# Feature-major products of a decoder layer as three 256-column matmuls a weight tile

## The chip, the cores and the metric

The kernel runs on one core of one Trainium2 chip. The metric is the device time of one execution in microseconds (us); the median of several runs is given. A profile is one further execution, with every engine's instructions recorded. TensorE is shown there as PE (matmuls) and PEld (weight loads), VectorE as DVE, ScalarE as ACT, GpSimd as POOL, SyncE as SP.

## The reference

One decoder layer on 256 tokens of width 2048, all in float32: a half-step SwiGLU feed-forward network (FFN) with layer norm, a token mixer, and a second such FFN.

```python
def swiglu(h, w_in, w_out):
    a, b = jnp.split(h @ w_in, 2, axis=-1)
    return (jax.nn.silu(a) * b) @ w_out

h = layer_norm(DN_ALPHA * h + 0.5 * swiglu(h, ffn1_w_in, ffn1_w_out), ln1_g, ln1_b)
q, k, v, qi, ki, wi, rx, rg, gates = split_cols(h @ w_in)
...                                              # rotary positions
y_attn = dsa_attention(q, k, v, qi, ki, wi)      # 16 heads, 64 keys chosen for each query
y_rnn = rglru_branch(rx, rg, conv_w, conv_b, wa, ba, wx, bx, lam)
g_attn, g_rnn = jnp.split(jax.nn.sigmoid(gates), 2, axis=-1)
merged = g_attn * (y_attn @ w_attn_branch) + g_rnn * (y_rnn @ w_rnn_branch)
h = layer_norm(DN_ALPHA * h + merged @ w_out, ln2_g, ln2_b)
h = layer_norm(DN_ALPHA * h + 0.5 * swiglu(h, ffn2_w_in, ffn2_w_out), ln3_g, ln3_b)
```

The FFN is 5632 wide, the recurrent branch 2560.

## The kernel before

Every weight is read once from HBM, in 1 MB chunks, and passes through TensorE once. For accuracy each float32 operand is kept as two float32r parts, high and low (`split`, and L108/L109 in `Weights.split_to` for the weights: ACT writes the high part `wh`, DVE the low part `wl`, 1024 columns at a time). A product is the sum of three partial products: high by high, high by low, low by high.

`Weights.unit` hands out the weight tiles in the order in which TensorE takes them. When a piece of 1024 columns (eight tiles of 128) is used up, it has the piece that is three further on split (`AHEAD` = 3, four buffers each for `wh` and `wl`), and lets one stage of the background work (`Background.step`: attention heads, rotary, indexer, recurrence) be emitted. The order of PE, SP and POOL is that of the program (`manual_schedule`); the order on ACT and DVE is planned by the framework from its own costs.

There are two kinds of product. Token-major ones (`blockA`; the output products and the q, k, v, qi projections) have the tokens as stationary operand and stream 512 weight columns: three matmuls of 512 columns (L446 to L448) for each of the two token halves. Feature-major ones have the 128x128 weight tile as stationary operand and stream the 256 tokens; their result is the next operand without a transpose. An activation tile `x` is 128 x 2 x 256: high part, then low part.

For the feature-major ones the kernel has two forms. `mmB` (L417, L418) streams high and low tokens together as 512 columns by the high weights, so that the two partial products lie side by side in a PSUM bank, and then the 256 high tokens by the low weights onto the first half. `sumB` then copies the second half to SBUF on ACT (L469) and adds the first half to it on DVE (L471). `mm3` (L831 to L833) has three matmuls of 256 columns that all accumulate in the first half of a bank; nothing is left to add.

Which product has which form: `mmB` with `pairB`, two banks at a time, in both FFNs' first products (1408 weight tiles each; the two sums go through Silu and a product, L600, L601, and a split, L475, L476); `mmB` with `blockB` in the ki projection (16 tiles), the two gates (256 tiles each: `ga` with Tanh at L797, `gr` at L883), the attention branch (256, on `ya`, L802) and the recurrent branch (320, on `yr`, L890, L891). `mm3` with `block3` in the recurrent inputs rx and rg (640 tiles on `hs`) and with `xc` in the two recurrent gates (104 tiles). The operands are `xs` in FFN 1 and `hs` behind a layer norm in the mixer and in FFN 2. PSUM has four banks for the products (`MM`) and four for the background work (`BP`).

Of the kernel before, what the change touches and what calls it, by code (L numbers as in the profile page):

```python
# [11 lines left out]
AF = mybir.ActivationFunctionType  # L12
OP = mybir.AluOpType
AX = mybir.AxisListType.X

P = 128
# [44 lines left out]


class Weights:
    """The weight stream: DMA of whole chunks, exact split of each piece into two float32r
    parts, and the units of the products in the order in which TensorE takes them."""

    def __init__(self, nc, pool, chunks, on_piece):
        self.nc, self.pool, self.chunks, self.on_piece = nc, pool, chunks, on_piece
# [58 lines left out]


class Background:
    """Work that is emitted a stage at a time between the pieces of the weight stream."""  # L130

    def __init__(self):
        self.lanes = {}
# [21 lines left out]


class Lazy:
    """The K tiles of an operand, emitted group by group, `ahead` groups before their use."""

    def __init__(self, n, per, make, ahead=1):  # L160
        self.n, self.per, self.make, self.ahead = n, per, make, ahead
# [14 lines left out]
def tile_layer(ctx, tc, x_fm, x_tm, pos, f1a, f1o, wA, wki, wB, lru, wab, wrb, wo, f2a, f2o,  # L176
# [66 lines left out]

    W = Weights(nc, pool, chunks, bg.step)

    # ---- start: x, constants
    xraw = [U("x") for _ in range(NK // 2)]

    def load_x_fm(k2):
# [128 lines left out]

    bg.add("main", later(consts(), W.last.ins))

    # ---- residual stream, token-major: Y[t][nb]
    Y = [[None] * 4 for _ in range(2)]

    def load_x():
# [27 lines left out]
                V.scalar_tensor_tensor(y, br, ALPHA, y, op0=OP.mult, op1=OP.add)  # L412
                yield

    # ---- products
    def mmB(ps, x, w, first, last):
        T.matmul(ps, w[0], x.rearrange("p a t -> p (a t)"), start=first, stop=False)  # L417
        T.matmul(ps[:, :S], w[1], x[:, 0], start=False, stop=last)  # L418

    def blockB(x):  # L420
        ps = MM()
        for k in range(len(x)):
            mmB(ps, x[k], W.unit(P), k == 0, k == len(x) - 1)
        return ps

    def pairB(x):
        pa, pb = MM(), MM()
        n = len(x)
        for h in range(2):
            for ps in (pa, pb):  # L430
                for k in range(h * n // 2, (h + 1) * n // 2):
                    mmB(ps, x[k], W.unit(P), k == 0, k == n - 1)
        return pa, pb

    def blockA(x, finish=None, lag=0, hold=False):
        """`finish`: the first half of the tokens runs ahead over the last pieces, and its sums
        are handed to it before the second half takes them. `hold`: the weights of the next
        product wait until the end of this one is on its way."""
        ps = [MM(), MM()]
        n = len(x)  # L440

        def half(t, k, w):
            wh, wl = w
            xh = x[k][:, 0, t * P:(t + 1) * P]
            xl = x[k][:, 1, t * P:(t + 1) * P]
            T.matmul(ps[t], xh, wh, start=k == 0, stop=False)  # L446
            T.matmul(ps[t], xh, wl, start=False, stop=False)  # L447
            T.matmul(ps[t], xl, wh, start=False, stop=k == n - 1)  # L448

        lead = 2 * lag  # L450
        ranges = [(k, k + 2) for k in range(0, n, 2)]
        if finish:
            ranges = ranges[:-lag] + [(n - lead, n)]
        for k0, k1 in ranges:
            ws = []
            for k in range(k0, k1):
                if hold and k == n - 2 * AHEAD:
                    W.spare = AHEAD
                ws.append(W.unit(512))
                half(0, k, ws[-1])  # L460
            if finish and k1 == n:
                finish(ps)
            for k in range(k0, k1):
                half(1, k, ws[k - k0])
        return ps

    def sumB(ps):
        t = T1()
        A.activation(t, ps[:, S:], AF.Copy)  # L469
        s = T1()  # L470
        V.tensor_tensor(s, ps[:, :S], t, op=OP.add)  # L471
        return s

    def split(dst, f):
        A.activation(dst[:, 0], f, AF.Copy)  # L475
# [31 lines left out]
            self.chained(t)  # L507

    class InnerNorm(Norm):
        """Layer norm whose result is the next operand, split and feature-major."""  # L510

        def __init__(self, gk, bk, g, b):
            self.gk, self.bk, self.g, self.b = gk, bk, g, b
# [28 lines left out]
            return hs  # L542

    class OuterNorm(Norm):
        """The last layer norm: its result leaves token-major."""

        last = True

# [23 lines left out]
                    nc.sync.dma_start(out[t * P:(t + 1) * P, nb * 512:(nb + 1) * 512], Y[t][nb])  # L572

    def out_product(x, ln):
        """Y += 0.5 x W; with `ln`, on to the statistics of the layer norm that follows."""

        def done(nb, ps, t):
            y_add(ps, nb, ln, t)
            if ln and nb == 3:
                ln.chain(t)  # L580

        for nb in range(4):
            if ln and nb == 3:
                ps = blockA(x, lambda ps: done(3, ps, 0), LAG_LAST if ln.last else LAG_LN, not ln.last)
                done(3, ps, 1)
            else:
                ps = blockA(x)
                for t in range(2):
                    done(nb, ps, t)
        if ln and ln.last:  # L590
            ln.finish()

    def ffn(x, ln):
        for s in range(SEG):
            g = []
            for j in range(NKS):
                pa, pb = pairB(x)
                sa = sumB(pa)
                sb = sumB(pb)
                A.activation(sa, sa, AF.Silu)  # L600
                V.tensor_tensor(sb, sa, sb, op=OP.mult)  # L601
                hl = UHL("g")
                split(hl, sb)
                g.append(hl)
            if s == SEG - 1:
                new_stats()
                ln.prepare()
            out_product(g, s == SEG - 1 and ln)

    # ==== FFN 1  # L610
    ln = InnerNorm("ln1_g", "ln1_b", ln1_g, ln1_b)
    ffn(xs, ln)
    hs = ln.hs

    # ==== mixer: token-major part of the input projection
    qT, kT, v, qiT = [None] * 8, [None] * 2, [None] * 2, [None] * 4
    kiT = C([P, S], "kiT")
    wi = C([P, 2, NIH], "wi")
# [154 lines left out]
        bg.add("head", head(h), 3)  # L773
    for b in a_order:
        if b is None:
            bg.add("rope", ki_task(sumB(blockB(hs))))
            for t in range(2):
                bg.add("rope", indexer(t))
            continue
        ps = blockA(hs)  # L780
        stg = stage(ps)
        if b >= 6:
            bg.add("rope", heads_T(stg, qiT, (b - 6) * 2, 8))
        elif b == 5:
            v[0], v[1] = stg
        elif b == 4:
            bg.add("qk", heads_T(stg, kT, 0, 16))
        else:
            bg.add("qk", heads_T(stg, qT, 2 * b, 16))
    # ==== attention gate, attention branch  # L790
    ga = []
    for j in range(NK):
        s = sumB(blockB(hs))
        if j % 2 == 0:
            u = U("ga")
        d = u[:, (j % 2) * S:(j % 2 + 1) * S]
        A.activation(d, s, AF.Tanh, scale=0.5)  # L797
        ga.append(d)
    bg.drain("rope", "qk", "head")
    for j in range(NK):  # L800
        s = sumB(blockB(ya))
        V.scalar_tensor_tensor(ga[j], ga[j], 1.0, s, op0=OP.add, op1=OP.mult)  # L802
    ya = None

    # ==== recurrent branch
    yr = [None] * NR

    def recur(g, tiles):
# [18 lines left out]
            yr[g * TPG + c] = hl  # L827
            yield

    def mm3(ps, x, w, first, last):  # L830
        T.matmul(ps[:, :S], w[0], x[:, 0], start=first, stop=False)  # L831
        T.matmul(ps[:, :S], w[0], x[:, 1], start=False, stop=False)  # L832
        T.matmul(ps[:, :S], w[1], x[:, 0], start=False, stop=last)  # L833

    def block3(x):
        ps = MM()
        for k in range(len(x)):
            mm3(ps, x[k], W.unit(P), k == 0, k == len(x) - 1)
        return ps[:, :S]

    xgs, xcs, tiles = {}, {}, []
    for j in range(NR + LAG):
        if j < NR:
# [13 lines left out]
        if j >= LAG:  # L857
            i = j - LAG
            g, c = divmod(i, TPG)
            pr, pi = MM(), MM()  # L860
            for ps in (pr, pi):
                ks = LRU_K[c]
                for n, k in enumerate(ks):
                    mm3(ps, xcs[g * TPG + k], W.unit(P), n == 0, n == len(ks) - 1)
            vw = U("vw")
            r, t = T1(), T1()
            A.activation(r, pr[:, :S], AF.Tanh, scale=0.5, bias=hba[:, i:i + 1])
            A.activation(t, pi[:, :S], AF.Tanh, scale=0.5, bias=hbx[:, i:i + 1])
            A.activation(vw[:, :S], r, AF.Tanh, scale=sp2[:, i:i + 1], bias=sp2[:, i:i + 1])
            V.scalar_tensor_tensor(xgs[i][:, :S], t, 1.0, xgs[i][:, :S], op0=OP.add, op1=OP.mult)  # L870
            tiles.append((xgs[i], vw))
            if c == TPG - 1:
                bg.add("rec", recur(g, tiles))
                tiles = []

    # ==== recurrent gate, recurrent branch, merge
    gr = []
    for j in range(NK):
        s = sumB(blockB(hs))
        if j % 2 == 0:  # L880
            u = U("gr")
        d = u[:, (j % 2) * S:(j % 2 + 1) * S]
        A.activation(d, s, AF.Tanh, scale=0.5)  # L883
        gr.append(d)
# [1 line left out]
    bg.drain("rec")  # L886
    mg = []
    for j in range(NK):
        s = sumB(blockB(yr))
        V.scalar_tensor_tensor(s, gr[j], 1.0, s, op0=OP.add, op1=OP.mult)  # L890
        V.tensor_tensor(s, s, ga[j], op=OP.add)  # L891
        hl = UHL("mg")
        split(hl, s)
        mg.append(hl)
    yr = None

    # ==== output projection
    new_stats()
    ln = InnerNorm("ln2_g", "ln2_b", ln2_g, ln2_b)
    out_product(mg, ln)  # L900
    mg = None

    # ==== FFN 2
    ffn(ln.hs, OuterNorm(ln3_g, ln3_b))


# [72 lines left out]
```

## Time and profile before

| | |
|---|---|
| median of 3 runs | 2487.92 us (2487.12 to 2487.92) |
| span of the profiled execution | 2489.5 us (first to last instruction; no other time of it is recorded) |
| mean granted TensorE clock | 0.996 |
| PE busy | 2458.6 us (99%), 13700 matmuls |
| PEld busy | 2122.5 us (85%), 13700 weight loads |
| DVE busy | 1502.6 us (60%) |
| ACT busy | 1267.8 us (51%) |
| read from HBM | 458.87 MB, 185 GB/s over the span |

In the profile's rows an instruction is shown with its line in the kernel, its engine, its operation, what it writes and reads (`mm<-hs,wh`: PSUM tile mm from hs and wh), and its shape; `x1936` is how many there are. A row of a group then has the busy time in us and the mean of one in ns, and behind the next bar the idle time of the engine just before these instructions with what ended it. A row of one line's instructions has the shortest, median and longest duration in ns and then the first and last start in us. A row of the waits has who waited for whom, then the total in us, the number and the longest. A row of the timeline has start and duration in us. Matmuls overlap, so a matmul's duration is longer than the distance between the starts of two.

### The profile page before, as it was taken

To read this page: it belongs to the slowest core of one execution; us is meant where nothing else is said; L and a number is where in the kernel's file an instruction comes from. 1 tells how busy PE (TensorE), PEld (TensorE's weight loads), DVE (VectorE), ACT (ScalarE), POOL (GpSimd) and SP (SyncE) were. 2 spreads that over 40 slices of the span, in tenths; PEclk is the share of its full clock that TensorE was granted. 3 is DMA by queue.
4 is the path that set the end of the run, shared out by engine and by line. 5 is a ranking of instruction groups with operands and counts; after the bars stand their busy time and mean duration, and the time that the engine had idled before them with its cause. 6 is when DMAs were issued, how large, how long until landed. Compare 5 with 4: busy or idle time off the path is not lost.

```text
span 2489.5 us, 33942 instructions
## 1 busy us (share of the span) xinstructions
PE 2458.6 (99%) x13700; PEld 2122.5 (85%) x13700; DVE 1502.6 (60%) x2106; ACT 1267.8 (51%) x1821; POOL 44.2 (2%) x74
## 2 busy tenths in 40 slices
PE   8999999999999999999999999999999999999997
PEld 7888888888887778888999988887888888888886
DVE  7555445555556676655788875655755544555555
ACT  5544434444335455544688874444554533544432
POOL 0000000000002000000000000002000000000001
PEclk9999999999999999999999999999999999999999
DMA  7655555555555444455555555555555556555553
GB/s 270 222 185 187 172 190 196 186 186 186 181 191 192 171 162 152 151 180 182 176 183 191 179 209 186 186 186 191 181 187 193 187 186 228 186 190 191 186 186 110
DMA packets 70557, 463.16 MB, mean 186 GB/s; under 512 B 8032, under 2 KB 8032, under 8 KB 17792
## 3 DMA queue, kind: packets, MB, share of 16 engines
q1 hardware_dynamic: 68400, 454.59, 52.2%
q0 software_dynamic: 2000, 6.41, 0.9%
q8 instruction: 107, 1.75, 0.3%
q14 instruction: 50, 0.41, 0.0%
HBM read 458.87 MB, written 2.10 MB: 185 GB/s over the span
## 4 chain that ended last, share of the span: by engine, by line
PE 97%; DVE 1%; ACT 1%; DMA 0%; POOL 0%; issue 0%; POOLq 0%; SPq 0%; DVEq 0%
PE mm L417 36%; PE mm L418 18%; PE mm L446 10%; PE mm L447 10%; PE mm L448 10%; PE mm L831 4%; PE mm L833 4%; PE mm L832 4%; ACT t L522 0%; PE bp L764 0%; PE bp L739 0%; PE bp L694 0%; DMA raw<-f1a 0%; PE bp L652 0%; PE bp L534 0%; DMA x<-x_fm 0%
## 5 line engine op out<-in xcount | busy, mean ns | idle before, releaser
L109 DVE TENSOR_TENSOR wl<-raw,wh 128x1024 fp32r<-128x1024 f32 (+2 forms) x860 | 1039.8, 1211 | 845.7 <-ACT wh L108 828.7
L108 ACT ACTIVATE wh<-raw 128x1024 fp32r<-128x1024 f32 (+2 forms) x866 | 908.5, 1050 | 993.0 <-PE mm L417 493.3
L417 PE MATMUL mm<-hs,wh 128*128 128x512 f32 x1936 | 680.4, 396 | 1.0 <-DVE hs L524 1.0
L418 PE MATMUL mm<-hs,wl 128*128 128x256 f32 x1936 | 543.2, 281 | 0.0
L417 PE MATMUL mm<-xs,wh 128*128 128x512 f32 x1408 | 499.9, 398 | 6.8 <-ACT wh L108 6.7
L417 PEld LDWEIGHTS mm<-hs,wh 128*128 128x128 f32 x1936 | 364.0, 188 | 84.6 <-DVE hs L524 2.0
L418 PE MATMUL mm<-xs,wl 128*128 128x256 f32 x1408 | 397.3, 282 | 0.8 <-DVE wl L109 0.8
L418 PEld LDWEIGHTS mm<-hs,wl 128*128 128x128 f32 x1936 | 364.9, 188 | 0.3
L417 PEld LDWEIGHTS mm<-xs,wh 128*128 128x128 f32 x1408 | 265.3, 188 | 72.9 <-ACT wh L108 6.7
L446 PE MATMUL mm<-wh,g 128*128 128x512 f32 x704 | 278.1, 395 | 0.0
L447 PE MATMUL mm<-wl,g 128*128 128x512 f32 x704 | 278.1, 395 | 0.0
L448 PE MATMUL mm<-wh,g 128*128 128x512 f32 x704 | 278.1, 395 | 0.0
L418 PEld LDWEIGHTS mm<-xs,wl 128*128 128x128 f32 x1408 | 266.4, 189 | 1.3 <-DVE wl L109 1.2
L831 PE MATMUL mm<-hs,wh 128*128 128x256 f32 x640 | 179.8, 281 | 0.0
L832 PE MATMUL mm<-hs,wh 128*128 128x256 f32 x640 | 179.8, 281 | 0.0
L833 PE MATMUL mm<-hs,wl 128*128 128x256 f32 x640 | 179.8, 281 | 0.0
L446 PEld LDWEIGHTS mm<-wh,g 128*128 128x128 f32 x704 | 132.0, 187 | 32.4
L448 PEld LDWEIGHTS mm<-wh,g 128*128 128x128 f32 x704 | 131.9, 187 | 32.3
L447 PEld LDWEIGHTS mm<-wl,g 128*128 128x128 f32 x704 | 132.0, 187 | 32.1
L471 DVE TENSOR_TENSOR t<-mm,t 128x256 f32<-128x256 f32 x241 | 101.3, 420 | 64.0 <-ACT t L469 63.9
L831 PEld LDWEIGHTS mm<-hs,wh 128*128 128x128 f32 x640 | 120.6, 188 | 0.1
L833 PEld LDWEIGHTS mm<-hs,wl 128*128 128x128 f32 x640 | 120.6, 188 | 0.0
(194 smaller groups left out, 2542.1 us busy)
## 6 DMA issues: line engine op xcount, KB each, us to landing
raw<-f2a SPq DMA_DIRECT2D x88, 1024.0 KB, 4.8
raw<-f1a SPq DMA_DIRECT2D x86, 1024.0 KB, 4.8
raw<-wB SPq DMA_DIRECT2D x72, 1024.0 KB, 4.8
raw<-f1o SPq DMA_DIRECT2D x40, 1024.0 KB, 4.9
raw<-f2o SPq DMA_DIRECT2D x40, 1024.0 KB, 4.9
raw<-wA SPq DMA_DIRECT2D x32, 1024.0 KB, 4.8
raw<-wrb SPq DMA_DIRECT2D x20, 1024.0 KB, 4.8
raw<-wab SPq DMA_DIRECT2D x16, 1024.0 KB, 4.8
```

The source lines that it names most:

```text
L108: nc.scalar.activation(h[:, q:e], src[:, q:e], AF.Copy)
L109: self.last = eng.tensor_tensor(l[:, q:e], src[:, q:e], h[:, q:e], op=OP.subtract)
L417: T.matmul(ps, w[0], x.rearrange("p a t -> p (a t)"), start=first, stop=False)
L418: T.matmul(ps[:, :S], w[1], x[:, 0], start=False, stop=last)
L446: T.matmul(ps[t], xh, wh, start=k == 0, stop=False)
L447: T.matmul(ps[t], xh, wl, start=False, stop=False)
L448: T.matmul(ps[t], xl, wh, start=False, stop=k == n - 1)
L471: V.tensor_tensor(s, ps[:, :S], t, op=OP.add)
L831: T.matmul(ps[:, :S], w[0], x[:, 0], start=first, stop=False)
L832: T.matmul(ps[:, :S], w[0], x[:, 1], start=False, stop=False)
L833: T.matmul(ps[:, :S], w[1], x[:, 0], start=False, stop=last)
```

## The change

All feature-major products take the `mm3` form. `mm3` and `block3` move up and return half a bank, `pair3` replaces `pairB`, and `mmB`, `blockB`, `pairB` and `sumB` go. What read the sum from SBUF now reads PSUM: Silu and the product with its result in the FFNs, Tanh in the gates, the gate products in the branches. For ki one copy to SBUF takes the place of `sumB`. Some comments are gone as well.

```diff
-    def mmB(ps, x, w, first, last):
-        T.matmul(ps, w[0], x.rearrange("p a t -> p (a t)"), start=first, stop=False)
-        T.matmul(ps[:, :S], w[1], x[:, 0], start=False, stop=last)
+    def mm3(ps, x, w, first, last):
+        T.matmul(ps, w[0], x[:, 0], start=first, stop=False)
+        T.matmul(ps, w[0], x[:, 1], start=False, stop=False)
+        T.matmul(ps, w[1], x[:, 0], start=False, stop=last)
...
-    def pairB(x):
-        pa, pb = MM(), MM()
+    def pair3(x):
+        pa, pb = MM()[:, :S], MM()[:, :S]
         n = len(x)
         for h in range(2):
             for ps in (pa, pb):
                 for k in range(h * n // 2, (h + 1) * n // 2):
-                    mmB(ps, x[k], W.unit(P), k == 0, k == n - 1)
+                    mm3(ps, x[k], W.unit(P), k == 0, k == n - 1)
         return pa, pb
...
-    def sumB(ps):
-        t = T1()
-        A.activation(t, ps[:, S:], AF.Copy)
-        s = T1()
-        V.tensor_tensor(s, ps[:, :S], t, op=OP.add)
-        return s
...
-                pa, pb = pairB(x)
-                sa = sumB(pa)
-                sb = sumB(pb)
-                A.activation(sa, sa, AF.Silu)
-                V.tensor_tensor(sb, sa, sb, op=OP.mult)
+                pa, pb = pair3(x)
+                sa = T1()
+                A.activation(sa, pa, AF.Silu)
+                V.tensor_tensor(sa, sa, pb, op=OP.mult)
                 hl = UHL("g")
-                split(hl, sb)
+                split(hl, sa)
...
-            bg.add("rope", ki_task(sumB(blockB(hs))))
+            s = T1("ki")
+            A.activation(s, block3(hs), AF.Copy)
+            bg.add("rope", ki_task(s))
...
-        s = sumB(blockB(hs))
+        s = block3(hs)
...
-        s = sumB(blockB(ya))
+        s = block3(ya)
         V.scalar_tensor_tensor(ga[j], ga[j], 1.0, s, op0=OP.add, op1=OP.mult)
...
-        s = sumB(blockB(yr))
-        V.scalar_tensor_tensor(s, gr[j], 1.0, s, op0=OP.add, op1=OP.mult)
+        s = T1()
+        V.scalar_tensor_tensor(s, gr[j], 1.0, block3(yr), op0=OP.add, op1=OP.mult)
         V.tensor_tensor(s, s, ga[j], op=OP.add)
```

More of the change, by code (lines that the diff above doesn't have):

```diff
@@ L413, in residual, with block3 @@
                 yield
-    def mmB(ps, x, w, first, last):
[L417 to L421, printed above, removed]
+    def mm3(ps, x, w, first, last):
+        T.matmul(ps, w[0], x[:, 0], start=first, stop=False)
+        T.matmul(ps, w[0], x[:, 1], start=False, stop=False)
+        T.matmul(ps, w[1], x[:, 0], start=False, stop=last)
+    def block3(x):
+        ps = MM()[:, :S]
         for k in range(len(x)):
-            mmB(ps, x[k], W.unit(P), k == 0, k == len(x) - 1)
+            mm3(ps, x[k], W.unit(P), k == 0, k == len(x) - 1)
         return ps
-    def pairB(x):
-        pa, pb = MM(), MM()
+    def pair3(x):
+        pa, pb = MM()[:, :S], MM()[:, :S]
         n = len(x)
@@ L828, in recur @@
             yield
[L830 to L839, printed above, removed]
     xgs, xcs, tiles = {}, {}, []
@@ L859, in tile_layer @@
             g, c = divmod(i, TPG)
-            pr, pi = MM(), MM()
+            pr, pi = MM()[:, :S], MM()[:, :S]
             for ps in (pr, pi):
@@ L866, in tile_layer @@
             r, t = T1(), T1()
-            A.activation(r, pr[:, :S], AF.Tanh, scale=0.5, bias=hba[:, i:i + 1])
-            A.activation(t, pi[:, :S], AF.Tanh, scale=0.5, bias=hbx[:, i:i + 1])
+            A.activation(r, pr, AF.Tanh, scale=0.5, bias=hba[:, i:i + 1])
+            A.activation(t, pi, AF.Tanh, scale=0.5, bias=hbx[:, i:i + 1])
             A.activation(vw[:, :S], r, AF.Tanh, scale=sp2[:, i:i + 1], bias=sp2[:, i:i + 1])
@@ L878, in tile_layer @@
     for j in range(NK):
-        s = sumB(blockB(hs))
+        s = block3(hs)
         if j % 2 == 0:
```

## The prediction

> **What bounds the kernel now.** I read the profile page first, for the busy shares and for the chain that ended last.
>
> ```profile
> span 2489.5 us, 33942 instructions
> PE 2458.6 (99%) x13700; PEld 2122.5 (85%) x13700; DVE 1502.6 (60%) x2106; ACT 1267.8 (51%) x1821; POOL 44.2 (2%) x74
> PE 97%; DVE 1%; ACT 1%; DMA 0%; POOL 0%; issue 0%; POOLq 0%; SPq 0%; DVEq 0%
> ```
>
> TensorE is the path: 97% of the chain is matmuls, and every other engine has at least 40% of its time free. The second view, the waits of the PE engine, says whether any of PE's idle time has to do with the copies and additions that the change removes.
>
> ```profile
> PE bp L534 <- DVE y L518: 8.2, 4, 3.2
> PE mm L417 <- ACT wh L108: 6.7, 1, 6.7
> PE mm L417 <- DVE hs L524: 1.0, 2, 0.5
> PE mm L418 <- DVE wl L109: 0.8, 1, 0.8
> PE bp L764 <- ACT pT L761: 0.4, 1, 0.4
> ```
>
> That is all of it, 17.1 us: the two layer norms (L534, L524), the first weights (L108, L109) and one attention head (L764). L469 and L471, the copy and the addition, are in none of these rows. What decides is therefore the pace of the matmul stream itself.
>
> The duration of a matmul in the trace is no pace, since matmuls overlap: a 128x512 one is shown with 392 ns or more. The pace is the distance from start to start. I took it from the third view, one line's instructions in a stage without other PE work: first and last start, over the count less one. One unit is the set of matmuls for one 128x128 weight tile, so consecutive starts of L417 (or of L831) are one unit apart. The rows below are, in this order, FFN 1 (two stretches), the gates, the attention branch, the recurrent branch, FFN 2 (two stretches); then the three-matmul form that the kernel already has (L831 on hs and on xc, one continuous stage); then L446, the token-major product, for three matmuls of 512 columns for each of two token halves.
>
> ```profile
> L417 PE MATMUL mm<-xs,wh x638: 392/397/402, 29.8 to 254.9; 128*128 128x512 f32 x160
> L417 PE MATMUL mm<-xs,wh x694: 392/397/402, 384.8 to 629.6; 128*128 128x512 f32 x174
> L417 PE MATMUL mm<-hs,wh x228: 392/397/402, 1439.8 to 1520.0; 128*128 128x512 f32 x114
> L417 PE MATMUL mm<-ya,wh x256: 392/397/402, 1081.0 to 1171.1; 128*128 128x512 f32 x128
> L417 PE MATMUL mm<-yr,wh x320: 392/397/402, 1526.0 to 1638.7; 128*128 128x512 f32 x160
> L417 PE MATMUL mm<-hs,wh x621: 392/392/392, 1759.8 to 1974.8; 128*128 128x512 f32 x156
> L417 PE MATMUL mm<-hs,wh x684: 392/392/392, 2114.9 to 2351.7; 128*128 128x512 f32 x171
> L831 PE MATMUL mm<-hs,wh x640: 277/280/285, 1171.4 to 1429.5; 128*128 128x256 f32 x160
> L831 PE MATMUL mm<-xc,wh x104: 277/280/285, 1205.5 to 1435.2; 128*128 128x256 f32 x104
> L446 PE MATMUL mm<-wh,mg x128: 393/396/398, 1639.0 to 1727.9; 128*128 128x512 f32 x128
> ```
>
> The two-matmul unit (512 columns, then 256): 225.1/637 = 353.4 ns, 244.8/693 = 353.2, 80.2/227 = 353.3, 90.1/255 = 353.3, 112.7/319 = 353.3, but in FFN 2 215.0/620 = 346.8 and 236.8/683 = 346.7. I use 353.3 outside FFN 2 and 346.7 in it. The three-matmul unit (256 columns each): 640 + 104 = 744 units from 1171.4 to 1435.2, 263.8/743 = 355.0 ns, or 118.3 a matmul. The token-major product: 88.9/127 = 700.0 ns for three matmuls of 512 columns twice, 233.3 a matmul.
>
> So 768 columns cost 353.3 or 346.7 ns in two matmuls and 355.0 in three. Why FFN 2 is quicker can be seen in the timeline but not explained from it: first FFN 1, then FFN 2.
>
> ```profile
> 500.32 0.40 PE L417 MATMUL mm<-xs,wh 128*128 128x512 f32 x1
> 500.56 0.28 PE L418 MATMUL mm<-xs,wl 128*128 128x256 f32 x1
> 500.68 0.39 PE L417 MATMUL mm<-xs,wh 128*128 128x512 f32 x1
> 500.91 0.28 PE L418 MATMUL mm<-xs,wl 128*128 128x256 f32 x1
> 501.03 0.40 PE L417 MATMUL mm<-xs,wh 128*128 128x512 f32 x1
> 1850.30 0.39 PE L417 MATMUL mm<-hs,wh 128*128 128x512 f32 x1
> 1850.53 0.28 PE L418 MATMUL mm<-hs,wl 128*128 128x256 f32 x1
> 1850.65 0.39 PE L417 MATMUL mm<-hs,wh 128*128 128x512 f32 x1
> 1850.88 0.28 PE L418 MATMUL mm<-hs,wl 128*128 128x256 f32 x1
> 1850.99 0.39 PE L417 MATMUL mm<-hs,wh 128*128 128x512 f32 x1
> ```
>
> In FFN 1 every second unit is longer (0.36, 0.35 us); in FFN 2 they are 0.35 and 0.34. The two-matmul stream falls into one of two steady patterns. The three-matmul stream has been seen in one only.
>
> **The change part by part.** Units first, from the counts of the page's groups.
>
> ```profile
> L417 PE MATMUL mm<-hs,wh 128*128 128x512 f32 x1936 | 680.4, 396 | 1.0 <-DVE hs L524 1.0
> L417 PE MATMUL mm<-xs,wh 128*128 128x512 f32 x1408 | 499.9, 398 | 6.8 <-ACT wh L108 6.7
> L832 PEld LDWEIGHTS mm<-hs,wh 128*128 128x128 f32 x640 | 120.6, 188 | 0.0
> L469 ACT ACTIVATE t<-mm 128x256 f32<-128x256 f32 x241 | 88.2, 366 | 3.3 <-PE mm L418 3.3
> L471 DVE TENSOR_TENSOR t<-mm,t 128x256 f32<-128x256 f32 x241 | 101.3, 420 | 64.0 <-ACT t L469 63.9
> L601 DVE TENSOR_TENSOR t<-t,t 128x256 f32<-128x256 f32 x88 | 37.4, 425 | 2.9
> ```
>
> The two-matmul units are 1408 (xs) + 1936 (hs) + 256 (ya) + 320 (yr) = 3920. FFN 2 has as many as FFN 1, so of hs 1408 are FFN 2's and 528 belong to the mixer; outside FFN 2 there are 3920 - 1408 = 2512.
>
> *The matmuls.* Each unit loses a 512-column matmul and gains two of 256, and a third weight load. The existing form loads the shared weights again for its second matmul (L832, 640 loads), so 3920 matmuls and 3920 loads are added, 17620 of each. All of it is on the path. At the pace of the existing form, loads included: outside FFN 2, 2512 x (355.0 - 353.3) = +4.3 us; in FFN 2, 1408 x (355.0 - 346.7) = +11.7 us; together +16.0 us. I take 355.0 in every stage since both streams of equal matmuls, 256 and 512 columns, showed one pace throughout, and only the mixed stream has two.
>
> The rows of equal matmuls give the price of cutting a 512-column matmul in two: 2 x 118.3 - 233.3 = 3.3 ns, or 3920 x 3.3 = 13.1 us if the mixed stream followed the same law; the step from 353.3 is smaller and that from 346.7 larger, and I take the measured steps. The Trainium skill (TensorE: Matmul & The Clock Gate, section "Wait — 56ns, not 53.3ns?") has a fixed cost of about 2.5 ns for every warm matmul beside its columns; by it alone, as an estimate, the cut costs 3920 x 2.5 = 9.8 us and the time is 2497.7. It speaks against the change as the rows do. The paces here, 118.3 and 233.3 ns, are above the 109.2 and 215.8 that its formula (columns / 2.4 plus 2.5) gives as an estimate, so the trace does not bear out its absolute figures for these operands.
>
> *The copy and the addition.* 241 copies (88.2 us of ACT) and 241 additions (101.3 us of DVE) go; one plain copy comes back for the ki product, and one T1 store is kept where the merge needs a place. Silu, Tanh, the gate product (L601) and the branch products now read PSUM. These lie beside PE, which waits for none of them, so the 189 us are worth nothing on the path. The bound of the gain is the 0.4 us of the attention row, whose chain shares ACT and DVE with the gate stage; I take -0.4. The start and the layer norms, with the other 16.7 us, contain none of these operations.
>
> *Waits.* The engines wait the same way in the new form: Silu waits for the last matmul of pa instead of a copy doing so, and the weight split (L108, L109) is queued behind it on ACT.
>
> ```profile
> ACT wh L108 <- PE mm L417: 493.3, 336, 3.1
> ACT t L600 <- DVE t L471: 117.1, 86, 3.2
> DVE wl L109 <- ACT wh L108: 828.7, 635, 2.9
> ```
>
> The split itself mostly waits for PE to free a buffer (493.3 us), so it is ahead of need; the split runs three pieces of eight units ahead, 3 x 8 x 355 ns = 8.5 us, against waits of at most 3.2. The 117.1 us wait of Silu for the addition goes; next on that chain is PE's own pace, so nothing follows. Cost 0, with 17 us of other PE idle untouched. A PSUM bank is held until Silu or the product has read it instead of the addition; there are four banks, two for each gate tile, so the next tile can run meanwhile, for 32 units or 11 us: 0 as well.
>
> Sum: +16.0 - 0.4 = +15.6 us. The profiled execution's span is 2489.5, 1.6 above the median of the runs (2487.92); I put the sum on the median: 2503.5.
>
> **The rivals.** *A fixed addition in every stage.* FFN 2's quicker pattern may belong to that stage and not to the mixed stream; then three-matmul units run there at 355.0 - 6.6 = 348.4 and every unit grows by 1.7: 3920 x 1.7 = 6.7 us, 2494.6. For it: the pattern held over both stretches of FFN 2, across a token-major product. Against: streams of equal matmuls show no second pattern.
>
> *A quicker pattern for three matmuls everywhere (faster).* If the new stream falls in FFN 1, mixer and FFN 2 alike into a pattern 6.6 ns below 355.0, then 2512 x (348.4 - 353.3) + 1408 x (348.4 - 346.7) = -12.3 + 2.4 = -9.9, less 0.4: 2477.6. It decides from a mean unit below (2512 x 353.3 + 1408 x 346.7)/3920 = 350.9 ns. For it: the mixed stream has such a pattern. Against: 744 units in a row at 355.0.
>
> *No change.* The quicker pattern is reached in some stages only, and the two signs cancel: within 5 us of 2487.9.
>
> *Weights late.* The order on ACT and DVE is planned, not written by hand; if each of the 88 gate tiles delayed the split past its lead of 8.5 us and PE then stood for one split, 88 x 1.2 (DVE's 1211 ns) = +106 us, 2609. Against it: ACT and DVE lose work.
>
> ```profile
> L109 DVE TENSOR_TENSOR wl<-raw,wh 128x1024 fp32r<-128x1024 f32 (+2 forms) x860 | 1039.8, 1211 | 845.7 <-ACT wh L108 828.7
> ```
>
> *Not what it says.* If the repeated load of the same weights were dropped, L832's loads would be missing already; they are there. I give this nothing of its own.
>
> **How the numbers follow.** Forecast 0.68 (2503.5), fixed addition 0.14 (2494.6), no change 0.08, quicker everywhere 0.07 (2477.6), weights late 0.03. A measurement of this kernel tells about 0.2% (5 us) from no change, so faster is 0.07, same 0.08, slower 0.68 + 0.14 + 0.03 = 0.85. Range: below, it takes in the fixed addition and the upper edge of no change, 2490; above, the forecast with a pattern half of 6.6 ns worse in one FFN, 1408 x 3.3 = +4.6, 2508. Left out: quicker everywhere 0.07, weights late 0.03, most of no change and a tail of the forecast 0.10.
>
> **What would show it.** Right: 17620 matmuls; units of 355.0 ns between L-starts in both FFNs and in the gates; FFN 2 longer by 11.7 us and FFN 1 by 2.4; PE's waits the same to about 1 us; DVE's busy time lower by about 101 us, ACT's by about 88. Wrong: a unit in FFN 2 near 348 (fixed addition), units below 351 in FFN 1 (quicker), or a row in which PE waits for L108 or L109 after the start (weights late).

## The result, and the profile after

The changed kernel takes 2506.91 us (median of 4 runs, 2505.66 to 2507.36) against 2487.92 (4 runs, 2487.12 to 2496.41): a ratio of 1.0067, 95% interval 1.005 to 1.0084. It is slower by 19.0 us between the medians; the forecast was 15.6. The spans of the two profiled executions, 2505.6 and 2489.5, are 16.1 us apart. (A run's time is 1.7 to 2.1 us above its span in every profile that has both, so the first profile's execution took about 2491.3 us, 3.4 above the median.)

The page of the changed kernel first: busy shares and chain.

```profile
span 2505.6 us, 41437 instructions
PE 2476.3 (99%) x17620; PEld 2317.6 (92%) x17620; DVE 1413.1 (56%) x1865; ACT 1187.5 (47%) x1581; POOL 44.2 (2%) x74
PE 98%; DVE 1%; DMA 0%; POOL 0%; ACT 0%; issue 0%; POOLq 0%; SPq 0%; DVEq 0%
```

17620 matmuls and loads, as counted. DVE is busy for 89.5 us less and ACT for 80.3, and the kernel is longer. All that PE waits for is this, 15.4 us, against 17.1 before:

```profile
PE bp L528 <- DVE y L512: 8.0, 4, 3.2
PE mm L417 <- ACT wh L108: 6.4, 1, 6.4
PE mm L419 <- DVE wl L109: 0.8, 1, 0.8
PE mm L418 <- DVE hs L518: 0.2, 1, 0.2
```

The pace is read as before, one line's first and last start in a stage (L417 is now the first of the three matmuls of a unit). Two stretches of FFN 1, two of FFN 2, the gates, the attention and the recurrent branch:

```profile
L417 PE MATMUL mm<-xs,wh x635: 276/281/286, 29.8 to 254.9; 128*128 128x256 f32 x159
L417 PE MATMUL mm<-xs,wh x691: 276/281/286, 384.8 to 629.8; 128*128 128x256 f32 x173
L417 PE MATMUL mm<-hs,wh x606: 277/281/286, 1760.0 to 1974.8; 128*128 128x256 f32 x152
L417 PE MATMUL mm<-hs,wh x658: 276/281/286, 2118.6 to 2351.8; 128*128 128x256 f32 x165
L417 PE MATMUL mm<-hs,wh x227: 277/281/286, 1439.7 to 1519.9; 128*128 128x256 f32 x114
L417 PE MATMUL mm<-ya,wh x256: 276/281/286, 1084.4 to 1174.9; 128*128 128x256 f32 x128
L417 PE MATMUL mm<-yr,wh x320: 276/281/286, 1530.2 to 1643.5; 128*128 128x256 f32 x160
```

225.1/634 = 355.0 ns, 245.0/690 = 355.1, 214.8/605 = 355.0, 233.2/657 = 354.9, 80.2/226 = 354.9, 90.5/255 = 354.9, 113.3/319 = 355.2: one pace everywhere, the one that the rows of the recurrent inputs gave before. With the pace before (353.3; in FFN 2 346.7) this is 16.0 of the 16.1 us between the two profiles.

### The profile page after: what moved, and what is told of

It reads as the page before. It is cut to its first block, busy times and chain, and to the rows that moved or that the text cites. A ratio compares the mean times of both kernels' runs of the same rounds, so it can differ in the third digit from the quotient of the medians.

```text
span 2505.6 us, 41437 instructions
## 1 busy us (share of the span) xinstructions
PE 2476.3 (99%) x17620; PEld 2317.6 (92%) x17620; DVE 1413.1 (56%) x1865; ACT 1187.5 (47%) x1581; POOL 44.2 (2%) x74
## 4 chain that ended last, share of the span: by engine, by line
PE 98%; DVE 1%; DMA 0%; POOL 0%; ACT 0%; issue 0%; POOLq 0%; SPq 0%; DVEq 0%
PE mm L418 22%; PE mm L419 22%; PE mm L417 22%; PE mm L447 10%; PE mm L449 10%; PE mm L448 10%; PE bp L528 0%; PE bp L732 0%; PE bp L757 0%; PE bp L687 0%; DMA raw<-f1a 0%; PE bp L645 0%; DMA x<-x_fm 0%; PE bp L751 0%; DVE y L479 0%; PE bp L731 0%
## 5 line engine op out<-in xcount | busy, mean ns | idle before, releaser
L109 DVE TENSOR_TENSOR wl<-raw,wh 128x1024 fp32r<-128x1024 f32 (+2 forms) x860 | 1039.1, 1210 | 949.5 <-ACT wh L108 939.4
L108 ACT ACTIVATE wh<-raw 128x1024 fp32r<-128x1024 f32 (+2 forms) x866 | 909.8, 1052 | 1231.5 <-PE mm L418 648.9
L417 PE MATMUL mm<-hs,wh 128*128 128x256 f32 x2576 | 728.2, 283 | 0.1
L418 PE MATMUL mm<-hs,wh 128*128 128x256 f32 x2576 | 725.3, 282 | 0.3 <-DVE hs L518 0.2
L418 PEld LDWEIGHTS mm<-hs,wh 128*128 128x128 f32 x2576 | 486.7, 189 | 1.2 <-DVE hs L518 0.9
L417 PEld LDWEIGHTS mm<-hs,wh 128*128 128x128 f32 x2576 | 486.7, 189 | 0.9 <-ACT hs L517 0.5
L417 PE MATMUL mm<-xs,wh 128*128 128x256 f32 x1408 | 397.6, 282 | 6.4 <-ACT wh L108 6.4
L418 PE MATMUL mm<-xs,wh 128*128 128x256 f32 x1408 | 397.3, 282 | 0.0
L417 PEld LDWEIGHTS mm<-xs,wh 128*128 128x128 f32 x1408 | 267.1, 190 | 6.8 <-ACT wh L108 6.4
L418 PEld LDWEIGHTS mm<-xs,wh 128*128 128x128 f32 x1408 | 267.0, 190 | 0.2 <-DVE xs L258 0.2
L447 PE MATMUL mm<-wh,hs 128*128 128x512 f32 x256 | 105.1, 411 | 0.0
L448 PE MATMUL mm<-wl,hs 128*128 128x512 f32 x256 | 101.5, 396 | 0.0
```

The lines of the kernel that those rows point to most:

```text
L108: nc.scalar.activation(h[:, q:e], src[:, q:e], AF.Copy)
L109: self.last = eng.tensor_tensor(l[:, q:e], src[:, q:e], h[:, q:e], op=OP.subtract)
L417: T.matmul(ps, w[0], x[:, 0], start=first, stop=False)
L418: T.matmul(ps, w[0], x[:, 1], start=False, stop=False)
```

## The experiments

Three questions were open. Is it the cutting of the matmul that costs, or accumulating in half a bank, or was something given back by ACT and DVE? Does the quicker pattern of FFN 2 belong to that stage? And what is the price of a further cut? One of the four runs of the kernel before, 2496.4, already stood 8.5 us above the other three, far more than the runs of the changed kernel scatter.

**The cut alone.**

```diff
-        T.matmul(ps, w[0], x.rearrange("p a t -> p (a t)"), start=first, stop=False)
+        T.matmul(ps[:, :S], w[0], x[:, 0], start=first, stop=False)
+        T.matmul(ps[:, S:], w[0], x[:, 1], start=False, stop=False)
```

> The kernel before with one edit: the 512-column matmul is cut into two of 256 columns, still into the two halves of a full bank, and the copy and the addition stay. My theory: the pace of the matmul stream is all there is, and 768 columns in three matmuls take 355.0 ns a unit in every stage, so this is as slow as the changed kernel, 2506.9 us, within 2 us. Rival, the half bank: the three matmuls cost more because all of them accumulate in the same 256 columns; then the units here stay near 350 and the time is below 2500. Rival, relief: dropping the copy and the addition gave the changed kernel a few us back; then this one is slower than 2509.

Measured: 2507.67 us (4 runs, 2506.98 to 2508.01), against the kernel before on the same chip 1.0069 (1.0051 to 1.0088). Its page, the attention head's wait and one stretch of FFN 1:

```profile
PE 2475.8 (99%) x17620; PEld 2315.7 (92%) x17620; DVE 1494.8 (60%) x2106; ACT 1255.5 (50%) x1819; POOL 44.3 (2%) x74
...
PE bp L765 <- ACT pT L762: 0.4, 1, 0.4
...
L417 PE MATMUL mm<-xs,wh x634: 277/280/285, 30.0 to 254.7; 128*128 128x256 f32 x159
```

224.7/633 = 355.0 ns with two half banks and with the copy and the addition in place. Neither the half bank nor the relief shows beyond the 0.8 us between this kernel and the changed one, which were not run side by side; the cut, with the load that comes with it, is the rest.

**No copy and no addition.** The FFNs, gates and branches read the first half of the bank, in the two-matmul form; ki keeps a copy. The second half, high weights by low tokens, is computed but left out of the result.

```diff
-        s = sumB(blockB(hs))
+        s = blockB(hs)[:, :S]
...
-                sa = sumB(pa)
-                sb = sumB(pb)
-                A.activation(sa, sa, AF.Silu)
-                V.tensor_tensor(sb, sa, sb, op=OP.mult)
+                sa = T1()
+                A.activation(sa, pa[:, :S], AF.Silu)
+                V.tensor_tensor(sa, sa, pb[:, :S], op=OP.mult)
```

> The kernel before with one edit: no copy and no addition, what read the sum reads the first half of the bank in PSUM (the product of the low token part is still computed but left out of the result). My theory: the copy and the addition lie beside TensorE, worth 0 to -0.5 us, 2487.9 within the scatter of the kernel before. Rival: the relief of ACT and DVE is worth 3 us or more, under 2485.

Measured: 2491.73 us (10 runs, 2482.07 to 2497.47) against 2489.06 (13 runs, 2481.89 to 2497.47) of the kernel before, ratio 1.0008 (0.9991 to 1.0026). No gain, as the theory had it; but both kernels scatter over 15 us, which no kernel whose feature-major products are all in three matmuls does (at most 1.7). The profile shows why. FFN 1's first and second half (the two stretches before and after the first output product), then FFN 2's first:

```profile
L417 PE MATMUL mm<-xs,wh x638: 392/397/402, 29.8 to 254.9; 128*128 128x512 f32 x160
L417 PE MATMUL mm<-xs,wh x659: 392/392/392, 399.7 to 627.8; 128*128 128x512 f32 x165
L417 PE MATMUL mm<-hs,wh x609: 392/392/402, 1759.9 to 1974.7; 128*128 128x512 f32 x153
```

225.1/637 = 353.4, 228.1/658 = 346.7, 214.8/608 = 353.3 ns. Here FFN 1's second half runs in the quick pattern and FFN 2 in the slow one, the reverse of the first profile. (A shortest and longest duration of 392 and 392 ns is the mark of the quick pattern; 392 and 402 that of the slow one.)

**The changed kernel with FFN 2 in the old form.** `ffn` takes `pairB` and `sumB` in its second call.

```diff
-    ffn(ln.hs, OuterNorm(ln3_g, ln3_b))
+    ffn(ln.hs, OuterNorm(ln3_g, ln3_b), True)      # pairB, sumB as before
```

> The changed kernel with FFN 2 alone in the old two-matmul form (with copy and addition). If the quick pattern of 346.7 ns a unit belongs to FFN 2 (its operands, its place in the program), this is 1408 x 8.3 ns = 11.7 us faster than the changed kernel, 2495.2, in every execution, with 346.7 in the trace. Rival: which pattern the two-matmul stream falls into is decided anew in each execution, as one run of the kernel before at 2496.4 beside three at 2487.9 hints; then the runs fall into two groups, near 2495.2 and near 2506.9 - 2.4 = 2504.5, and the trace shows 346.7 or 353.3.

Measured: 2504.46 us (4 runs: 2505.5, 2500.9, 2504.43, 2504.48), not 2495.2. FFN 2 in the profile of the first of them:

```profile
L437 PE MATMUL mm<-hs,wh x610: 392/397/402, 1759.6 to 1974.8; 128*128 128x512 f32 x153
L437 PE MATMUL mm<-hs,wh x657: 392/392/402, 2119.9 to 2351.7; 128*128 128x512 f32 x165
```

215.2/609 = 353.4 and 231.8/656 = 353.4 ns. The quick pattern does not belong to FFN 2. (2500.9, 3.5 us below the other runs' 2504.4, may be a run with one quick half; it has no profile.)

**The kernel before, profiled again.**

> The kernel before, unchanged, for a second profile. If the pattern belongs to the stage: 353.3 ns a unit everywhere but in FFN 2, 346.7 there, as in the first profile. Rival: the pattern is decided in each execution; then some stage shows the other value than in the first profile.

Measured: 2502.4 us, span 2500.6. FFN 2, where the first profile had 346.7:

```profile
L417 PE MATMUL mm<-hs,wh x610: 392/397/402, 1759.8 to 1975.0; 128*128 128x512 f32 x153
L417 PE MATMUL mm<-hs,wh x672: 392/396/402, 2114.8 to 2351.9; 128*128 128x512 f32 x168
```

215.2/609 = 353.4, 237.1/671 = 353.4: the same program, the same stage, the other pattern. 11.1 us separate the spans of the two profiles of one kernel. A half of an FFN is 704 units, and 704 x 6.7 ns = 4.7 us, so the two halves are 9.4 of them; the rest came before 30 us, where the granted clock averaged 0.94 here and 1.00 in the first profile. All 48 runs of the kernel before that stand beside this study's runs fall into groups about that far apart: 5 from 2481.9 to 2484.9, 15 from 2486.1 to 2489.1, 17 from 2490.8 to 2493.5, 9 from 2495.7 to 2498.2, 2 at 2501.9. That these are four, three, two, one and no quick halves fits the profiles (none quick: 2502.4; one quick, in the kernel without sums: 2497.5; two quick, in the first profile: about 2491.3); for the runs without a profile it is an inference, and four would need a quick first half of FFN 1, which no profile shows.

**More cuts.** A different set of matmuls in each half of the two FFNs, 704 units each.

```diff
+    forms = [mm_128lo, mm_six, mm_384, mm_alt]
+    # mm_128lo: w[0] on x[:, 0] (256), w[0] on x[:, 1] twice 128, w[1] on x[:, 0] (256)
+    # mm_six: the same three products in six matmuls of 128
+    # mm_384: w[0] on 384 and on 128 of the 512 columns, w[1] on x[:, 0] (256)
+    # mm_alt: w[0], w[1], w[0], three of 256
-                    mm3(ps, x[k], W.unit(P), k == 0, k == n - 1)
+                    mm(ps, x[k], W.unit(P), k == 0, k == n - 1)
```

> The changed kernel with another set of matmuls for each unit in each half of the two FFNs (704 units each): FFN 1 first half, the middle 256-column matmul cut into two of 128; FFN 1 second half, all three cut, six of 128; FFN 2 first half, 384 + 128 columns of high and low tokens together and then 256 (the low part lands in the second half of the bank, which is left out of the result); FFN 2 second half, the three of 256 in another order, so that no two neighbours have the same weights. Theory, a price for each matmul: 233.3 ns for 512 columns and 118.3 for 256 make 3.3 ns a matmul and 0.449 ns a column, so the units take 358.3, 365.0, 355.0 and 355.0 ns and the time is 704 x (3.3 + 10.0) = 9.4 us above the changed kernel's, 2516. Rival, the weight load: a load takes a fixed time of its own, near the 108 ns between the 128-column transposes, which the 256-column matmul just covers; then the units take about 118 + 2 x 108 + 118 = 452, 6 x 108 = 648, 176 + 108 + 118 = 402 and 355 ns, and the time is 704 x (97 + 293 + 47) = 308 us longer, 2815.

Measured: 2837.88 us, one run. The rival, the weight load, was near with 2815; my price for each matmul and column fails below 256 columns. The rows, in the order of the four halves:

```profile
L422 PE MATMUL mm<-xs,wh x435: 280/281/288, 100.1 to 299.8; 128*128 128x256 f32 x145
L430 PE MATMUL mm<-xs,wh x1195: 273/274/275, 500.0 to 699.9; 128*128 128x128 f32 x200
L435 PE MATMUL mm<-hs,wh x346: 333/338/344, 2059.7 to 2200.0; 128*128 128x384 f32 x173
L440 PE MATMUL mm<-hs,wh x423: 277/280/285, 2449.9 to 2599.7; 128*128 128x256 f32 x141
```

199.7/434 = 460.1 ns a unit; L430 on `wh` is four of the six, 199.9/1194 x 4 = 669.7 ns; 140.3/345 = 406.7; 149.8/422 = 355.0. The six matmuls of 128 columns are 111.6 ns apart. The matmul itself does not need this: in the first half, where two of 128 columns follow each other (L423, L424 below), the starts are some 60 ns apart. That leaves the load before each. (The Trainium skill, TensorE: Matmul & The Clock Gate, section "LDWEIGHTS (loading the stationary operand)", puts a load at columns / 1.2 ns, 106.7 as an estimate for 128; the distance here is 5 ns above it.)

```profile
150.37 0.22 PE L423 MATMUL mm<-xs,wh 128*128 128x128 f32 x1
150.43 0.27 PE L424 MATMUL mm<-xs,wh 128*128 128x128 f32 x1
```

With 111.6 ns for each matmul of 128 columns, the first half comes to 118.3 + 2 x 111.6 + 118.3 = 459.8, against 460.1 measured. A matmul of 256 columns, 118.3 ns, covers such a load with 6.7 ns to spare. The fourth half, with no two neighbours on the same weights, has 355.0 as well: loading the same weights again is neither cheaper nor dearer. The sum of the four, 704 x (105.1 + 314.7 + 51.7 + 0) = 331.9 us, accounts for the 331.0 above the changed kernel.

**Another order.** The same matmuls as before; of 8, 2, 4 and 2 units first the 512-column ones, then the 256-column ones.

```diff
-                    mmB(ps, x[k], W.unit(P), k == 0, k == n - 1)
+                for k0 in range(h * n // 2, (h + 1) * n // 2, m):      # m = 8, 2, 4, 2
+                    ws = []
+                    for k in range(k0, k0 + m):
+                        ws.append(W.unit(P))
+                        T.matmul(ps, ws[-1][0], x[k].rearrange("p a t -> p (a t)"), start=k == 0, stop=False)
+                    for k in range(k0, k0 + m):
+                        T.matmul(ps[:, :S], ws[k - k0][1], x[k][:, 0], start=False, stop=k == n - 1)
```

> The kernel before with the same matmuls in another order in the FFNs: of 8 units first the 512-column matmuls and then the 256-column ones (FFN 1 first half), of 2 units (second half), of 4 (FFN 2 first half), of 2 (second half). Theory: the two patterns of 353.3 and 346.7 come from the strict alternation of 512 and 256 columns; in long runs of equal length each length has its own pace, and the unit takes 233.3 + 118.3 = 351.7 ns in groups of 8 in any execution, and something between in shorter groups. Rival: the pattern is a state of the whole execution that has nothing to do with the order; then each half shows 353.3 or 346.7.

Measured: 2496.56 us, one run. The row covers whole groups of 8, from the start of one to the start of another:

```profile
L439 PE MATMUL mm<-xs,wh x617: 395/396/396, 30.6 to 247.2; 128*128 128x512 f32 x155
```

216.6/616 = 351.6 ns, the sum of the two paces, 233.3 + 118.3; the other halves have 351.3 (groups of 2) and 350.8 (groups of 4) between the starts of whole groups. So in this profile neither of the two patterns stands without strict alternation, and from 351.6 to 355.0 the cut costs 3.4 ns, as the rows of equal matmuls say (3.3).

**Disturbing the pattern.** Could the quick pattern be had every time? Every 32 units three units were put in another order, or a matmul was cut; a different kind in each half.

```diff
+    # one of these at the units 3 to 5 of each pair; H: 512 columns, L: 256 of the low weights
+    # e7: H H L L | H L L H | one H cut in two | H H H L L L
+    # e9: H H H L L L | H H L H L L | H L L L H H | H L L L L H L with one H cut in two
```

> The kernel before with one small disturbance in each pair of FFN columns (every 32 units), among the units 3 to 5: FFN 1 first half, two units in the order 512, 512, 256, 256 columns; second half, 512, 256, 256, 512; FFN 2 first half, one 512-column matmul cut into two of 256; second half, three units in the order 512 x 3, 256 x 3. Theory: the pattern is chosen anew behind each disturbance, by where in the pattern the disturbance falls, so each kind leads to one pattern again and again (346.7 or 353.3 ns a unit between the disturbances), and a kind that leads to 346.7 makes a kernel that is faster than both, down to 2502.4 - 2816 x 6.7 ns = 2483.6 us for all four halves. Rival: the pattern is fixed by something outside the stream (the granted clock's pauses, the stage); then each half keeps one pattern behind all its 22 disturbances, and the time lies in the range of the kernel before, 2482 to 2502.

Measured: 2495.78 us, one run. The last of the four, three 512-column matmuls in a row, left its half in the quick pattern behind each of its 22 disturbances; the other three halves were slow behind each of theirs. The first half of FFN 1 and the second of FFN 2:

```profile
L417 PE MATMUL mm<-xs,wh x579: 392/395/402, 29.8 to 255.0; 128*128 128x512 f32 x193
L417 PE MATMUL mm<-hs,wh x620: 392/392/392, 2114.9 to 2351.7; 128*128 128x512 f32 x155
```

By the theory the row of three was therefore worth putting everywhere, except in the first pair of each half, so that the entry could be seen:

```diff
+                    if first or not (h == 0 and ps is pa) or k not in (3, 4, 5):
+                        mmB(ps, x[k], ws[-1], k == 0, k == n - 1)
+                    elif k == 5:
+                        # 512 columns of units 3, 4, 5, then their 256 columns
```

> The kernel before with the disturbance behind which the quick pattern stood (three 512-column matmuls in a row, then their three of 256) in every pair of FFN columns but the first of each half, and in every column block of the gates and branches. Theory: this disturbance leads to 346.7 ns a unit from any pattern; then each FFN half turns from 353.3 (or 346.7) to 346.7 behind its first disturbance, the gates and branches too, and the time is near 2502.4 - (2750 + 1000) x 6.7 ns = 2477 us in every execution, faster than both kernels. Rival: the disturbance only leaves the pattern as it is, and the half in which it was tried had begun in the quick one; then the time scatters like that of the kernel before, 2482 to 2502 us, with a median near 2490.

> Other disturbances, each at every pair of FFN columns of one half, the first included: FFN 1 first half, the three in a row as before; second half, 512, 512, 256, 512, 256, 256; FFN 2 first half, 512, 256, 256, 256, 512, 512; second half, 512, 256, 256, 256, 256, 512, 256 (one 512-column matmul cut). If a disturbance leads to a pattern of its own, the three in a row give 346.7 ns in FFN 1 too, where no profile of the kernel before has shown it in the first half. If it only leaves the pattern as it is, FFN 1's first half stays at 353.3.

Measured: the row of three everywhere 2488.88 us (12 runs, 2483.55 to 2491.09) against 2490.76 (17 runs, 2482.42 to 2498.16), ratio 0.9992 (0.9978 to 1.0006): no difference shown, and no 2477. The four halves of its profile:

```profile
L417 PE MATMUL mm<-xs,wh x579: 389/392/402, 29.8 to 254.9; 128*128 128x512 f32 x193
L417 PE MATMUL mm<-xs,wh x635: 392/392/392, 384.7 to 626.8; 128*128 128x512 f32 x159
L417 PE MATMUL mm<-hs,wh x551: 389/392/402, 1760.9 to 1974.0; 128*128 128x512 f32 x184
L417 PE MATMUL mm<-hs,wh x621: 392/392/392, 2114.7 to 2351.9; 128*128 128x512 f32 x156
```

The second and fourth are quick from their undisturbed first pair on, the first and third slow to the end, with the same disturbances in all. In the second kernel (2496.08 us, one run) the row of three left FFN 1's first half slow, and 512, 512, 256, 512, 256, 256 kept the second half quick. The theory fell for the row of three: it leaves either pattern as it is.

Not every disturbance does. The first units of a half, before any disturbance, already tell the pattern. Below: the first three units of FFN 1's second half in the first kernel with disturbances, and its units behind the first disturbance (512, 256, 256, 512); then the first four units of a quick half (first profile) and of a slow one (second profile) of the kernel before.

```profile
L417 PE MATMUL mm<-xs,wh x3: 392/392/397, 382.0 to 382.7; 128*128 128x512 f32 x3
L417 PE MATMUL mm<-xs,wh x29: 392/395/402, 384.1 to 394.0; 128*128 128x512 f32 x29
L417 PE MATMUL mm<-hs,wh x4: 392/392/397, 2108.4 to 2109.4; 128*128 128x512 f32 x4
L417 PE MATMUL mm<-xs,wh x4: 393/396/398, 384.3 to 385.3; 128*128 128x512 f32 x4
```

That half was entered quick and was slow behind its first disturbance. FFN 2's second half in the second kernel (512, 256, 256, 256, 256, 512, 256) went the same way. No disturbance was seen to turn slow into quick.

The sign of the pattern is older than the half. From start to start, the token-major stream before a second half repeats four distances, about 231, 235, 233 and 234 ns. The traces have 15 second halves with alternating matmuls. Before the eight that were entered quick, the short distance is the last or last but one of that stream; before the seven entered slow, it is the third from the end. What sets this rhythm's place, and what decides behind a layer norm, was not found; of the seven halves that stayed quick, one was a first half behind a layer norm.

**The opposite of the change.** If a cut costs 1.7 to 8.3 ns, the products that were in three matmuls from the beginning should gain from the two-matmul form.

```diff
-            s = block3(hs)
+            s = sumB(blockB(hs))
...
-            A.activation(xg[:, S:], block3(hs), AF.Gelu_apprx_tanh)
+            A.activation(xg[:, S:], sumB(blockB(hs)), AF.Gelu_apprx_tanh)
```

> The opposite of the change: the kernel before with its 40 products rx and rg (640 units on hs) in the two-matmul form too, with 40 more copies and additions. By the paces of a unit, 640 x (355.0 - 353.3) = 1.1 us faster than the kernel before if the slow pattern holds there, 640 x 8.3 = 5.3 us if the quick one does. Rival, ACT and DVE become the bound: in this stage they are busy 194.5 and 192.0 of 240 us, and 40 x 0.366 us and 40 x 0.420 us are added, so they come to about 209 of 240; if the weight split then comes late, PE shows waits for L108 or L109 there and the time is the same as before or longer.

Measured: 2506.9 us (7 runs, 2500.7 to 2514.96) against 2493.11 (12 runs, 2486.99 to 2501.88), ratio 1.0058 (1.0038 to 1.0078): slower. The busy time of the engines within the stage, and PE's waits:

```profile
1185.00:1425.00 240.00, 234.02 (x1395) 204.70 (x1394) 192.42 (x293) 206.86 (x322) 0.00 (x0) 1.00 0.52 174
...
PE mm L418 <- DVE wl L109: 7.4, 10, 0.9
PE mm L831 <- ACT xc L475: 1.9, 1, 1.9
PE mm L832 <- DVE xc L476: 0.5, 1, 0.5
```

The columns are PE, PEld, DVE, ACT. ACT is busy for 207 of 240 us, from 1300 to 1400 us for 90.7 of 100, and the split of the weights (L109) comes too late nine times in this stage (6.6 us; the tenth wait, 0.8, is the one at the start). The rival holds: where ACT and DVE are this full, the copy and the addition are on the path, and the form without them is the better one. Whether the fullness makes the split late, or the order planned for ACT and DVE, was not separated.

The waits named in this stage, some 9 us, are less than the 13.8 between the medians, but the distances between starts account for it. From its first start to that of the next gate the stage takes 1449.5 - 1171.6 = 277.9 us, against 1435.5 - 1171.4 = 264.1 in the first profile of the kernel before, 13.8 more (first this kernel, then the first gate of the kernel before):

```profile
L417 PE MATMUL mm<-hs,wh x641: 387/392/503, 1171.6 to 1449.5; 128*128 128x512 f32 x161
L417 PE MATMUL mm<-hs,wh x2: 393/395/397, 1435.5 to 1435.9; 128*128 128x512 f32 x2
```

A wait is counted only from the shown end of the matmul before it, so the stream loses more than the rows of waits say. About 1.7 us of it, as an estimate, is the granted clock of 0.83 from 1440 to 1450 us (10 x 0.17). This profile is of the slowest of the seven runs, with all four FFN halves slow.

## Why the prediction was right, and where it was not

**The pace of three matmuls.** Predicted 355.0 ns in every stage because streams of equal matmuls had shown one pace. Measured 354.9 to 355.2 in all seven stretches. This is the step that carried the forecast, and the rival of a quicker pattern for three matmuls fell with it.

**The count.** 3920 more matmuls and loads: 17620, as the page shows. DVE was to be busy for 101 us less and ACT for 88; the page has 89.5 and 80.3, since it counts the time of overlapping instructions once. Summed one by one, the durations in the traces fall by 103 and 94 us.

**The sum.** Against the first profile, FFN 2 was to grow by 11.7 us; 1408 x (355.0 - 346.7) by the rows after is the same. The rest of the path was to grow by 4.3; the spans differ by 16.1 in all, with the forecast at 16.0 before the relief.

**The pattern in FFN 2.** This step was wrong in its reason. The prediction took 353.3 outside FFN 2 and 346.7 in it as what the kernel before does; the second profile and the kernel with FFN 2 in the old form showed that it was what one execution did. The term that depends on it is 4.7 us for each quick half. By the units, against an execution with no quick half the change costs 3920 x 1.7 = 6.7 us, against one with two 16, with three about 21. The prediction took the size of the term from one execution, of about 2491.3 us, and put it on the median of others, 2487.92: these 3.4 us are the difference between the forecast of 15.6 and the 19.0 measured. That the median is a run of three quick halves, as its group suggests, fits their sign and order. How near the forecast came is in part luck: with the second profile, where no half is quick, the same working gives 6.7 us before the relief, or 2494.6. And the 5 us by which the prediction would tell a change from none is too little for one run of this kernel, which varies by 20. The rival of a fixed addition of 1.7 ns in each stage fell as it was put, though it gives the right cost against an execution without quick halves.

**The relief.** Forecast -0.4 us. The attention head's wait of 0.4 us, there with only the cut (L765), is gone in the changed kernel, as forecast. The kernel with only the cut is 0.8 us slower than the changed one, of that order, and the one without sums shows no gain that its scatter lets one see. The copy and the addition were beside the path, as said; the last experiment shows the cover that this rests on: with ACT at 81% of a stage, 80 more small operations there are no longer free.

**Weights late.** It did not happen in the changed kernel: PE's wait for L108 and L109 stayed at 7.2 us, all at the start.

## What to carry to other kernels

Where the matmul stream is the path, read its pace from start to start and price an edit in matmuls, columns and loads; a copy and an addition on engines that are half idle were worth nothing that these runs show, and a matmul cut in two costs its own few nanoseconds, thousands of times. Look at the room in the very stage before applying this the other way: in a stage with ACT and DVE near 80% the sums were on the path. And take a second profile before a forecast rests on a difference of 2% between two stages that do the same.

## What the runs showed of the hardware

A stream that alternates matmuls of 512 and 256 columns runs at 353.3 or at 346.7 ns for the pair, and one of the two holds for a whole stretch of 704 undisturbed pairs; three long and then three short, 22 times a half, left it as it was, and two other changes of order turned quick into slow. Streams of equal matmuls (118.3 ns for 256 columns, 233.3 for 512) and grouped ones (351.6 ns) have one pace. One program's time varied by 20 us, 2481.9 to 2501.9, at granted clocks of 0.994 to 0.997. With a 128-column weight load before each, matmuls of 128 columns followed each other at 111.6 ns, nearly the 118.3 of 256 columns.
